# Order of VectorE's work in the seven-product up stage of a hybrid layer, with one operand kept in DRAM a second time

## The chip, the cores and the metric

The kernel runs on one core of a Trainium2 chip. The metric is the device time of one execution in microseconds (us), as the median of several runs; lower is better. TensorE (PE) multiplies matrices into PSUM; VectorE (DVE), ScalarE (ACT) and GpSimd (POOL) work element by element; SyncE (SP) issues most of the transfers between DRAM and on-chip memory (SBUF). Each engine works through its own list of instructions in a fixed order; where an instruction needs the result of another engine, it waits, and everything behind it on that engine waits too.

## What is computed

One decoder layer on 512 tokens of width 1024: two token mixers side by side (RWKV-7 time mixing and a sparse attention), gates, an output projection, and then a gated MLP. The change lies in the MLP, which is the last part:

```python
h = rms_norm(x, norm_ffn_pre[l])
u = causal_dwconv(h @ ffn_up[l], ffn_conv_w[l], ffn_conv_b[l])
u_gate, u_val = jnp.split(u, 2, axis=-1)
x = x + rms_norm((jax.nn.silu(u_gate) * u_val) @ ffn_down[l], norm_ffn_post[l])
```

`ffn_up` is 1024 x 5632, `ffn_down` 2816 x 1024; the convolution goes over three neighbouring tokens of each channel.

## The kernel before, in words

**Precision.** Each float32 operand of a product is split into a high part (rounded by a ScalarE copy to the matmul's format) and a low part (operand minus high part, one subtraction). A product is then three matmuls: high by high, low by high, high by low. So every weight tile costs a load (SP), a copy (ACT) and a subtraction (POOL or DVE: `split_to`, L166 to L172), and every activation tile a copy and a subtraction.

**The up stage** (L1593 to L1652) runs over 22 steps j, each of which makes 128 gate channels and 128 value channels of `u` for all 512 tokens, then the product y = silu(gate) * value, whose high part goes to `ah[:, j]` (L1638, ACT) and whose low part goes to `al[:, j]` (L1639, DVE). For j = 0 to 9 a step is two plain products. For j = 10 to 21 (`SEVEN`) the function `seven(j)` computes the 2 x 2 block product of a step with seven half-size products instead of eight. Each of the seven (`prod`, L1562) is 12 matmuls of 256 columns, and takes one weight tile from the list `ahead`. They go into the accumulators `sg` (gate), `sv` (value) and two temporary ones `st` (`t[0]`, `t[1]`), all in PSUM, and VectorE combines them between the products (`add`, L1571, whose line all the combining rows of the profile carry).

Two of the seven share `t[1][:, rgt]`: the fourth product is written there, VectorE reads it in `add(v[:, rgt], t[1][:, rgt], u4)` (L1584), and the seventh product, with `forms[3]` (L1587), is then accumulated on top of it. So TensorE may not start the seventh product of a step before that addition is done. The text calls this addition **the gate**; in the profile it is the first `sv<-st,su` of a step, and TensorE's row behind it is the first `st<-tf3h`.

**Weights of the seven products.** `form_w` (L1538) loads a tile, makes its high part and its low part. Of the seven tiles of a step five have their low part on POOL, and two on VectorE: the ones whose names end in 1 (`sw171`) and in 8 (`sw178`); the digits in front are the j. `coming` makes one more tile after each product, five tiles ahead of TensorE (L1615).

**What comes behind a step.** y's step runs on while the products of the next j are under way: convolution on ACT and DVE (L1619 to L1621), silu, y (L1635), `ah`, `al`. The down stage does the same trick with seven products over 2 x 2 blocks: its steps pair channel block j with block j + 11 (`KH` = 11). For j < 11 the right half of y is replaced by right minus left (L1637); the text calls that half T1 of block j. For j >= 11 VectorE also makes two token sums of 256 columns each and stores them in `t24d`: y's right half minus T1, and y's left half minus that. T1 is put together again from its two parts, so that the first sum takes two instructions: minus the high part (L1647), minus the low part (L1648); L1649 is the second sum.

**What sets the order.** The kernel's code gives the program order; a scheduling layer orders the instructions of each engine by it and by its own estimates, except where `keep` (keep in program order) pins an instruction. The buffers are rings: a load into a ring's slot waits until its last reader is done.

**The down stage** (L1655 on) works through 77 weight tiles `dw0` to `dw76`; the first ten are begun ahead of it. The raw tile of `dw8` and `dw9` lies in the pool `t2`, those from `dw10` on mostly in the pool `ep` in the tag `draw`.

Of the kernel before, what the change touches and what calls it, by code (L numbers as in the profile page):

```python
# [52 lines left out]
def hybrid_layer(ctx: ExitStack, tc: tile.TileContext, a, out, dbg=None, stop=None):  # L53
# [207 lines left out]

    t24d = dr.tile([KH, 128, S], F32, name="t24d", bufs=1)
# [1216 lines left out]
    with pool("ff") as ff:  # L1479
# [58 lines left out]
        def form_w(src, name, eng):  # L1538
            n = next(ring)
            p_, tags, b = (wp, ("raw", "whi", "wlo"), (RAWB, WB)) if n % 8 % 3 == 1 else (sw, ("sraw", "shi", "slo"), (4, 5))  # L1540
            hi = p_.tile([128, 512], F32R, tag=tags[1], name=name + "h", bufs=b[1])
            lo = p_.tile([128, 512], F32R, tag=tags[2], name=name + "l", bufs=b[1])
            split_to(src, hi, lo, name, 512, eng, p_, late=n < 5, tag=tags[0], bufs=b[0])
            return hi, lo

# [12 lines left out]
        def seven(j):  # L1558
# [3 lines left out]
            def prod(p, x, first=True, last=True):  # L1562
# [6 lines left out]
                next(coming, None)  # L1569

# [13 lines left out]
            add(v[:, rgt], t[1][:, rgt], u4)  # L1584
            prod(g[:, rgt], tok(1, 1))
            add(g[:, rgt], g[:, rgt], u4, OP.subtract)
            prod(t[1][:, rgt], forms[3], first=False)  # L1587
            add(v[:, lft], t[1][:, rgt], u2)
            return g, v

        side = token_forms()
        sctx2 = ExitStack()
        for j in range(22):  # L1593
# [45 lines left out]
            ve.tensor_tensor(al[:, j, :], y, ah[:, j, :].bitcast(F32), op=OP.subtract)  # L1639
            if j >= KH:  # L1640
                if j == KH:
                    t2ctx = ExitStack()
                    t2 = pool("t2", "left", t2ctx)
                else:
                    sy.dma_start(t24d[j - 1 - KH], t24)
                t24 = t2.tile([128, S], F32, tag="t24", name=f"t24{j}", bufs=2)
                ve.tensor_tensor(t24[:, lft], y[:, rgt], ah[:, j - KH, rgt].bitcast(F32), op=OP.subtract)  # L1647
                ve.tensor_tensor(t24[:, lft], t24[:, lft], al[:, j - KH, rgt].bitcast(F32), op=OP.subtract)  # L1648
                ve.tensor_tensor(t24[:, rgt], y[:, lft], t24[:, lft], op=OP.subtract)  # L1649
            if j == 1:  # L1650
                f4ctx.close()
        po.dma_start(t24d[21 - KH], t24)  # L1652
        ring = itertools.count()

        def down_w(f, k):  # L1655
# [8 lines left out]
            elif n < 10:  # L1664
                raw = t2.tile([128, 512], F32, tag="draw", name=f"dw{n}r", bufs=2)
            else:
                raw = ep.tile([128, 512], F32, tag="draw", name=f"dw{n}r", bufs=4)
# [12 lines left out]
        with pool("ep") as ep:  # L1680
# [3 lines left out]
            g3 = ep.tile([128, D], F32, name="gb4")  # L1684
            s2, x2 = {}, {}
# [233 lines left out]
```

## Time and profile before

| | |
|---|---|
| median of 3 runs | 1137.9 us (1136.57 to 1139.19) |
| the profiled execution: its time, and the span of its trace | 1133.54 us, 1131.5 us |
| granted TensorE clock, mean | 0.997 |
| busy share of the span: PE, DVE, ACT, POOL | 98%, 66%, 56%, 54% |
| DMA: moved, mean rate | 208.33 MB, 184 GB/s |

The page of the profile gives per engine the busy time; the groups of instructions by line, engine and tile (`sw171l<-sw171r,sw171h` is the low part of tile sw171, made from the raw tile and its high part); the waits (who waited, for whom); the chain of work that ended last; and, on request, the instructions in order of time and the busy times in any stretch. Times within the trace count from the start of the span. A row of the timeline has start, duration, engine, line, operation, tiles and shape, and in brackets the idle time ahead of it with what ended it. Rows of VectorE overlap by some 0.08 us, since the next instruction starts before the last one has drained; what an instruction costs its engine is the distance from its start to the next start.

### The profile page before, as it was taken

The numbers are of one execution on the slowest core, as the hardware profiler recorded it, in microseconds if no ns is written. First come the engines' busy times: TensorE is split into PE (matmuls) and PEld (weight loads), VectorE is DVE, ScalarE is ACT, GpSimd is POOL, SyncE is SP. The second block draws the span as 40 slices with busy tenths as digits, with TensorE's granted clock in tenths as the row PEclk, the third lists the DMA queues.
The fourth block names the chain that finished last, engine by engine and source line by source line (L and its number), as shares of the span: only waits on it lengthen the run. The fifth ranks groups of instructions, "written<-read, shape, count | busy, mean of one in ns | idle before, by whom it ended". The sixth has DMA issues, their size and how long they took to land.

```text
span 1131.5 us, 21237 instructions
## 1 busy us (share of the span) xinstructions
PE 1110.3 (98%) x7704; PEld 909.6 (80%) x7704; DVE 750.4 (66%) x1432; ACT 639.2 (56%) x1258; POOL 613.5 (54%) x615
## 2 busy tenths in 40 slices
PE   9999999999999999999999999999999999999997
PEld 7888888877888887766666777888888899998885
DVE  4236664735666552597787754755785699997986
ACT  6447763554666434386675654543554576665554
POOL 4346674535666453566545543540578777753431
PEclk9999999999999999999999999999999999999999
DMA  7524468632666896516576465777568678968783
GB/s 256 144 81 124 141 166 217 182 104 86 182 146 172 235 242 216 132 48 194 171 218 181 127 149 166 231 240 220 136 185 202 207 263 227 266 181 302 228 283 113
DMA packets 117002, 208.33 MB, mean 184 GB/s; under 512 B 37025, under 2 KB 39905, under 8 KB 110754
## 3 DMA queue, kind: packets, MB, share of 16 engines
q1 hardware_dynamic: 93538, 144.05, 40.6%
q0 software_dynamic: 7504, 48.50, 18.4%
q10 hardware_dynamic: 15856, 14.42, 4.0%
q8 instruction: 61, 1.00, 0.4%
q14 instruction: 43, 0.35, 0.1%
HBM read 179.60 MB, written 72.35 MB: 223 GB/s over the span
## 4 chain that ended last, share of the span: by engine, by line
PE 87%; DVE 5%; DMA 3%; POOL 2%; issue 1%; ACT 1%; SPq 0%; DVEq 0%; POOLq 0%; ACTq 0%
PE st L1567 4%; PE sg L1567 3%; PE dn L1745 3%; PE dn L1746 3%; PE dn L1747 3%; PE gt L348 3%; PE o L1218 3%; PE gt L349 3%; PE gt L350 3%; PE pt L150 3%; PE ub L1276 3%; PE pu L234 2%; PE ub L1278 2%; PE pu L232 2%; PE pu L233 2%; PE ub L1277 2%
## 5 line engine op out<-in xcount | busy, mean ns | idle before, releaser
L1166 ACT ACTIVATE p<-p,stt 128x384 f32<-128x384 f32 (+3 forms) x128 | 70.6, 554 | 33.4 <-DVE stt L1164 30.8
L1164 DVE CUSTOM_DVE_ANT_0 p<-s,rh 128x384 f32<-128x384 f32 (+3 forms) x128 | 59.2, 484 | 21.5 <-PE s L1150 17.9
L1138 POOL TENSOR_SCALAR p<-p,stt 128x512 f32<-128x512 f32 (+1 forms) x64 | 39.3, 622 | 38.7 <-DVE stt L1131 24.5
L1746 PE MATMUL dn<-hl,ah 128*128 128x512 f32 x148 | 57.6, 389 | 0.0
L1747 PE MATMUL dn<-hh,al 128*128 128x512 f32 x148 | 57.6, 389 | 0.0
L1745 PE MATMUL dn<-hh,ah 128*128 128x512 f32 x148 | 57.2, 389 | 0.0
L150 PE MATMUL pt<-ident,p 128*128 128x128 f32 x320 | 44.3, 273 | 1.2 <-DVE p L1140 1.2
L1157 PE MATMUL s<-kst,qs 128*128 128x512 f32 (+1 forms) x128 | 38.8, 394 | 5.8 <-DVE stt L1164 5.6
L150 PEld LDWEIGHTS pt<-ident,p 128*128 128x128 f32 x320 | 37.8, 141 | 6.9 <-DVE p L1140 1.6
L1218 PE MATMUL o<-PT,vt 128*64 128x384 f32 (+3 forms) x256 | 41.0, 443 | 0.0
L1209 ACT ACTIVATE PT<-pt 128x512 f32<-128x512 f32 x48 | 27.5, 587 | 10.4 <-PE pt L150 10.3
L1157 PEld LDWEIGHTS s<-kst,qs 128*128 128x128 f32 x128 | 21.2, 189 | 15.0 <-DVE stt L1164 11.8
L1140 DVE TENSOR_SCALAR p<-p,stt 128x512 f32<-128x512 f32 (+1 forms) x64 | 32.3, 532 | 0.7
L1747 PEld LDWEIGHTS dn<-hh,al 128*128 128x128 f32 x148 | 27.8, 188 | 5.8
L1745 PEld LDWEIGHTS dn<-hh,ah 128*128 128x128 f32 x148 | 27.8, 188 | 5.8
L1746 PEld LDWEIGHTS dn<-hl,ah 128*128 128x128 f32 x148 | 27.8, 188 | 5.7
L1218 PEld LDWEIGHTS o<-PT,vt 128*64 128x64 f32 x256 | 16.3, 136 | 18.3 <-issue 16.0
L272 POOL DMA_DIRECT2D ds<-in_down_dram x36 | 25.6, 710 | 7.3 <-DMA ds<-ds 7.3
L1620 DVE SCALAR_TENSOR_TENSOR u<-pu,cvec,u 128x511 f32<-128x511 f32 x20 | 15.0, 748 | 19.2 <-ACT u L1619 19.2
L1211 DVE COPY PT<-pt 128x512 f32<-128x512 f32 x32 | 21.8, 680 | 8.6 <-PE pt L150 8.5
L251 POOL DMA_DIRECT2D fs<-in_up_dram x36 | 26.0, 731 | 0.5 <-issue 0.4
L868 ACT ACTIVATE UV<-xs 64x256 f32<-64x256 f32 x16 | 6.0, 378 | 35.7 <-PE xs L861 35.3
(2206 smaller groups left out, 4242.4 us busy)
## 6 DMA issues: line engine op xcount, KB each, us to landing
fs<-in_up_dram POOLq DMA_DIRECT2D x36, 512.0 KB, 6.5
ds<-in_down_dram POOLq DMA_DIRECT2D x30, 512.0 KB, 6.1
fs<-fs POOLq DMA_DIRECT2D x12, 512.0 KB, 4.4
ds<-ds POOLq DMA_DIRECT2D x10, 512.0 KB, 5.7
gtd<-gt ACTq DMA_DIRECT2D x16, 256.0 KB, 4.8
qs<-qd SPq DMA_DIRECT2D x32, 128.0 KB, 3.6
g<-gtd SPq DMA_DIRECT2D x16, 256.0 KB, 3.6
t24d<-t SPq DMA_DIRECT2D x10, 256.0 KB, 5.4
```

Source lines behind the costliest of these rows:

```text
L150: return te.transpose(o, i, ident)
L348: te.matmul(p, wh(k), hh[:, k, :], start=k == 0, stop=False)
L349: te.matmul(p, wh(k), hl[:, k, :], start=False, stop=False)
L1138: po.tensor_scalar(o.pe[e, b, k], o.pe[e, b, k], w, 1.0, op0=OP.mult, op1=OP.mult)
L1157: m = te.matmul(s_[:, :n], qt, kt[:, x, b, :n], start=x == 0, stop=x == 1)
L1164: ve.tensor_tensor_reduce(sb, parts[b], rh[e][:, (3 - qb) * 128:], -1.0, BIG, OP.add, OP.min, st[e][:, 0, i:i + 1])
L1166: sc.activation(sb, sb, AF.Exp, scale=-1.0, bias=st[e][:, 0, i:i + 1], accum_out=st[e][:, 1, i:i + 1])
L1218: te.matmul(acc[e * 64:e * 64 + 64, j * 128:], vt[:, j, b * 256 + g * 64:b * 256 + g * 64 + 64], m[e][:, c:c + n], start=False, stop=k == ...
L1567: te.matmul(p, w[y][:, ks], x[z][:, k, :], start=first and k + n == 0, stop=last and k == hf - 1 and n == 2, skip_group_check=True)
L1745: te.matmul(p, xh, w[0], start=first, stop=False)
L1746: te.matmul(p, xh, w[1], start=False, stop=False)
L1747: te.matmul(p, xl, w[0], start=False, stop=last)
```

## The change

- `form_w`: where a low part is VectorE's, the load and the high part are issued as before, but the low part is put on a list `lows`; `flush()` issues what is on it. `flush` is called twice in a step: behind the gate and behind the last reader of `t[1]`.
- `al` and the token sums of a step are put on a list `deferred`. `settle()` issues them, in the next step behind the gate; where the step is not one of `SEVEN`, or is the last, at once.
- T1 of each block j < 11 is also stored in float32 in a DRAM buffer `t1d` (a store of 128 KB on ACT's queue), and loaded again by SP into a ring of two tiles `t1`, two blocks ahead of its use. The first token sum is then one instruction, y's right half minus this tile.
- `coming` makes one tile more per product in j = 10, until seven tiles are ahead.
- The raw tiles of `dw8` and `dw9` lie in the pool `sw` instead of `t2`; in `ep` the tile `p2jk` is laid out ahead of `draw`, so that the `draw` tiles lie elsewhere.

```diff
@@ form_w
-            split_to(src, hi, lo, name, 512, eng, p_, late=n < 5, tag=tags[0], bufs=b[0])
+            if n < 5 or eng is po:
+                split_to(src, hi, lo, name, 512, eng, p_, late=n < 5, tag=tags[0], bufs=b[0])
+            else:
+                raw = p_.tile([128, 512], F32, tag=tags[0], name=name + "r", bufs=b[0])
+                sy.dma_start(raw, src)
+                sc.activation(hi, raw, AF.Copy)
+                lows.append((lo, raw, hi))
             return hi, lo
+
+        lows = []
+
+        def flush():
+            while lows:
+                lo, raw, hi = lows.pop(0)
+                keep(ve.tensor_tensor(lo, raw, hi.bitcast(F32), op=OP.subtract))
@@ prod
                 next(coming, None)
+                if j == SEVEN[0] and len(ahead) < 7:
+                    next(coming, None)
@@ seven
             add(v[:, rgt], t[1][:, rgt], u4)
+            settle()
+            flush()
             prod(g[:, rgt], tok(1, 1))
             add(g[:, rgt], g[:, rgt], u4, OP.subtract)
             prod(t[1][:, rgt], forms[3], first=False)
             add(v[:, lft], t[1][:, rgt], u2)
+            flush()
             return g, v
+
+        hold, deferred = [], []
+
+        def t1_load(k):
+            t = hold[0].tile([128, 256], F32, tag="t1", name=f"t1{k}", bufs=2)
+            sy.dma_start(t, t1d[k])
+            return t
+
+        def settle():
+            while deferred:
+                j, y = deferred.pop(0)
+                ve.tensor_tensor(al[:, j, :], y, ah[:, j, :].bitcast(F32), op=OP.subtract)
+                if j >= KH:
...
+                    else:
+                        sy.dma_start(t24d[j - 1 - KH], hold[2])
+                    t24 = hold[2] = hold[0].tile([128, S], F32, tag="t24", name=f"t24{j}", bufs=2)
+                    ve.tensor_tensor(t24[:, lft], y[:, rgt], hold[3 + j - KH], op=OP.subtract)
+                    if j < 20:
+                        hold.append(t1_load(j - KH + 2))
+                    ve.tensor_tensor(t24[:, rgt], y[:, lft], t24[:, lft], op=OP.subtract)
@@ the loop over j
-            ve.tensor_tensor(al[:, j, :], y, ah[:, j, :].bitcast(F32), op=OP.subtract)
-            if j >= KH:
...
-                t24 = t2.tile([128, S], F32, tag="t24", name=f"t24{j}", bufs=2)
-                ve.tensor_tensor(t24[:, lft], y[:, rgt], ah[:, j - KH, rgt].bitcast(F32), op=OP.subtract)
-                ve.tensor_tensor(t24[:, lft], t24[:, lft], al[:, j - KH, rgt].bitcast(F32), op=OP.subtract)
-                ve.tensor_tensor(t24[:, rgt], y[:, lft], t24[:, lft], op=OP.subtract)
+            if j < KH:
+                tc.keep_in_program_order(sc.dma_start(t1d[j], y[:, rgt]))
+            deferred.append((j, y))
+            if sv_ is None or j == 21:
+                settle()
@@ down_w
-                raw = t2.tile([128, 512], F32, tag="draw", name=f"dw{n}r", bufs=2)
+                raw = sw.tile([128, 512], F32, tag="sraw", name=f"dw{n}r", bufs=4)
@@ the pool ep
+            ep.tile([128, 512], F32, tag="p2jk", name="p2jk", bufs=1)
```

TensorE's list is the same instruction for instruction. What moves stands here at two engines.

VectorE, before, while the products of j = 16 are under way and y of j = 15 is finished. `su` are the combining tiles u2 and u4 in SBUF, `t` is the token sum, the last two rows belong to the next turn:

```order
L1635 TENSOR_TENSOR sv_10748<-u_10890,sg_10747 128x512
L1572 TENSOR_TENSOR su_10908<-sv_10904,su_10907 128x256
L172 TENSOR_TENSOR sw171l<-sw171r,sw171h 128x512
L1639 TENSOR_TENSOR al<-sv_10748,ah 128x512
L1647 TENSOR_TENSOR t_10899<-sv_10748,ah 128x256
L1572 TENSOR_TENSOR sv_10904<-st_10906,su_10908 128x256
L1648 TENSOR_TENSOR t_10899<-t_10899,al 128x256
L1649 TENSOR_TENSOR t_10899<-sv_10748,t_10899 128x256
L1572 TENSOR_TENSOR sg_10903<-sg_10903,su_10908 128x256
L172 TENSOR_TENSOR sw178l<-sw178r,sw178h 128x512
L1620 SCALAR_TENSOR_TENSOR u_11041<-sg_10903,cvec,u_11041 128x511
```

VectorE, now, at the same place; L1588 is the line of `add`, L1620 that of `al`, L1630 and L1633 the token sums, L1558 the low parts:

```order
L1679 TENSOR_TENSOR sv_10773<-u_10922,sg_10772 128x512
L1588 TENSOR_TENSOR su_10934<-sv_10930,su_10933 128x256
L1620 TENSOR_TENSOR al<-sv_10773,ah 128x512
L1588 TENSOR_TENSOR sv_10930<-st_10932,su_10934 128x256
L1630 TENSOR_TENSOR t_11030<-sv_10773,t_10718 128x256
L1633 TENSOR_TENSOR t_11030<-sv_10773,t_11030 128x256
L1558 TENSOR_TENSOR sw171l<-sw171r,sw171h 128x512
L1588 TENSOR_TENSOR sg_10929<-sg_10929,su_10934 128x256
L1664 SCALAR_TENSOR_TENSOR u_11074<-sg_10929,cvec,u_11074 128x511
L1588 TENSOR_TENSOR sv_10930<-st_10932,su_10933 128x256
L1558 TENSOR_TENSOR sw178l<-sw178r,sw178h 128x512
```

Ahead of the gate (`sv<-st,su`) the low part of sw171 and the first token sum are gone, and `al` still stands there. One of the three token instructions is gone. The low part of sw178 has gone behind the second `sv<-st,su`, so that nothing stands any more between `sg<-sg,su` and the convolution's first instruction on `sg`.

SyncE, before, around the store of a token sum:

```order
L168 DMA sw164r<-fs_129 128x512
L168 DMA sw162r<-fs_127 128x512
L168 DMA sw163r<-fs_128 128x512
L168 DMA sw175r<-in_up_dram 128x512
L1645 DMA t24d<-t_10587 128x512
L168 DMA sw173r<-fs_128 128x512
L168 DMA sw166r<-in_up_dram 128x512
```

SyncE, now:

```order
L168 DMA sw164r<-fs_129 128x512
L168 DMA sw162r<-fs_127 128x512
L168 DMA sw175r<-in_up_dram 128x512
L1614 DMA t_10718<-t1d 128x256
L1628 DMA t24d<-t_10716 128x512
L168 DMA sw163r<-fs_128 128x512
L168 DMA sw166r<-in_up_dram 128x512
L168 DMA sw173r<-fs_128 128x512
```

The load of T1 stands directly ahead of the store; the load of sw163 has gone behind both.

More of the change, by code (lines that the diff above doesn't have):

```diff
@@ L260, in weight_sums @@
                     yield
+    t1d = dr.tile([KH, 128, 256], F32, name="t1d", bufs=1)
     t24d = dr.tile([KH, 128, S], F32, name="t24d", bufs=1)
@@ L1588, in seven @@
             add(v[:, lft], t[1][:, rgt], u2)
+            flush()
             return g, v
+        hold, deferred = [], []
[8 more added lines that the diff above has]
+                if j >= KH:
+                    if j == KH:
+                        t2ctx = ExitStack()
+                        hold[:] = [pool("t2", "left", t2ctx), t2ctx, None]
+                        t1s = hold + [t1_load(0), t1_load(1)]
+                        hold[:] = t1s
+                    else:
[5 more added lines that the diff above has]
+                    ve.tensor_tensor(t24[:, rgt], y[:, lft], t24[:, lft], op=OP.subtract)
         side = token_forms()
@@ L1638, in hybrid_layer @@
             sc.activation(ah[:, j, :], y, AF.Copy)
-            ve.tensor_tensor(al[:, j, :], y, ah[:, j, :].bitcast(F32), op=OP.subtract)
-            if j >= KH:
[L1641 to L1645, printed above, removed]
-                t24 = t2.tile([128, S], F32, tag="t24", name=f"t24{j}", bufs=2)
-                ve.tensor_tensor(t24[:, lft], y[:, rgt], ah[:, j - KH, rgt].bitcast(F32), op=OP.subtract)
-                ve.tensor_tensor(t24[:, lft], t24[:, lft], al[:, j - KH, rgt].bitcast(F32), op=OP.subtract)
-                ve.tensor_tensor(t24[:, rgt], y[:, lft], t24[:, lft], op=OP.subtract)
+            if j < KH:
[3 more added lines that the diff above has]
+                settle()
             if j == 1:
                 f4ctx.close()
+        t2, t2ctx, t24 = hold[:3]
         po.dma_start(t24d[21 - KH], t24)
```

## The prediction

> **What bounds the kernel now.** I read the page first: which engine is full.
>
> ```profile
> PE 1110.3 (98%) x7704; PEld 909.6 (80%) x7704; DVE 750.4 (66%) x1432; ACT 639.2 (56%) x1258; POOL 613.5 (54%) x615
> ```
>
> TensorE is the bound, and its work isn't changed. An edit on VectorE can only bring what TensorE loses by waiting in that stage. So next come the busy times in stretches: first the steps of the stage, each cut at TensorE's first matmul of a step (j = 10 starts at 898.91), then the whole stage and the down stage. Behind each stretch stand its length, the busy time of PE, its weight loads, DVE, ACT and POOL with the number of instructions, TensorE's clock, the DMA engines' share and GB/s.
>
> ```profile
> 898.91:908.63 9.72, 9.72 (x85) 9.71 (x84) 7.92 (x12) 6.31 (x11) 7.22 (x6) 1.00 0.78 244
> ...
> 928.15:937.84 9.69, 9.69 (x87) 9.69 (x85) 9.23 (x17) 6.94 (x13) 7.08 (x6) 1.00 0.80 256
> ...
> 968.19:978.82 10.63, 10.02 (x86) 9.82 (x85) 10.28 (x17) 7.30 (x14) 8.18 (x7) 1.00 0.93 262
> 978.82:988.50 9.68, 9.68 (x86) 9.68 (x85) 8.54 (x17) 6.55 (x13) 5.33 (x5) 1.00 0.93 266
> ...
> 898.91:1018.99 120.08, 118.40 (x1009) 117.51 (x1008) 111.97 (x185) 80.27 (x141) 84.04 (x68) 1.00 0.79 235
> 1018.99:1121.20 102.21, 102.21 (x453) 84.65 (x452) 85.12 (x100) 58.47 (x102) 37.99 (x25) 1.00 0.70 239
> ```
>
> The first four steps take (937.84 - 898.91) / 4 = 9.73 us, which is TensorE's own pace, 1.39 for each of the seven products. Twelve would take 116.8; the stage takes 120.08. So 3.3 us are lost, at a clock of 1.00, in the steps from j = 14 on; with the shortest step, 9.68, it would be 120.08 - 116.2 = 3.9. This is the most that the change can bring. The down stage loses nothing. VectorE is busy for 112 of the 120 us: a few tenths more per step and it is the bound. Who holds TensorE up stands in the waits and in TensorE's rows at j = 16:
>
> ```profile
> PE st L1567 <- DVE sv L1572: 1.6, 3, 0.7
> 964.73 0.28 PE L1567 MATMUL sg<-hh,sw164h 128*128 128x256 f32 x1
> 966.05 0.28 PE L1567 MATMUL sg<-hh,sw164l 128*128 128x256 f32 x1
> 966.68 0.39 PE L1567 MATMUL st<-tf3h,sw168h 128*128 128x256 f32 x1 [0.35 <-DVE sv L1572]
> ```
>
> The seventh product should follow at 966.17 and starts at 966.68, behind the gate. What VectorE did until then:
>
> ```profile
> 959.62 0.42 DVE L1572 TENSOR_TENSOR sv<-st,su 128x256 f32<-128x256 f32 x1
> 959.95 0.73 DVE L1621 SCALAR_TENSOR_TENSOR u<-sg,cvec,u 128x510 f32<-128x510 f32 x1
> 960.88 0.75 DVE L1620 SCALAR_TENSOR_TENSOR u<-sv,cvec,u 128x511 f32<-128x511 f32 x1 [0.20 <-ACT u L1619]
> ...
> 962.66 0.69 DVE L1635 TENSOR_TENSOR sv<-u,sg 128x512 f32<-128x512 f32 x1
> 963.26 0.42 DVE L1572 TENSOR_TENSOR su<-sv,su 128x256 f32<-128x256 f32 x1
> 963.59 1.76 DVE L172 TENSOR_TENSOR sw171l<-sw171r,sw171h 128x512 fp32r<-128x512 f32 x1
> 965.27 0.68 DVE L1639 TENSOR_TENSOR al<-sv,ah 128x512 fp32r<-128x512 f32 x1
> 965.88 0.41 DVE L1647 TENSOR_TENSOR t<-sv,ah 128x256 f32<-128x256 f32 x1
> 966.21 0.41 DVE L1572 TENSOR_TENSOR sv<-st,su 128x256 f32<-128x256 f32 x1
> 966.54 0.41 DVE L1648 TENSOR_TENSOR t<-t,al 128x256 f32<-128x256 f32 x1
> 966.98 0.42 DVE L1649 TENSOR_TENSOR t<-sv,t 128x256 f32<-128x256 f32 x1
> 967.32 0.42 DVE L1572 TENSOR_TENSOR sg<-sg,su 128x256 f32<-128x256 f32 x1
> 968.27 1.37 DVE L172 TENSOR_TENSOR sw178l<-sw178r,sw178h 128x512 fp32r<-128x512 f32 x1 [0.53 <-ACT sw178h L134]
> 969.57 0.73 DVE L1620 SCALAR_TENSOR_TENSOR u<-sg,cvec,u 128x511 f32<-128x511 f32 x1
> 970.23 0.41 DVE L1572 TENSOR_TENSOR sv<-st,su 128x256 f32<-128x256 f32 x1
> ```
>
> The gate (966.21) could have run at 963.6: the fourth product was done by 963.4, since the fifth and sixth, 1.39 each, come behind it. Ahead of it stand a low part of 1.68, `al` and a token sum. The whole turn, 959.62 to 970.23, is 10.61 us, longer than TensorE's 9.73. The gate ends at 966.62, when TensorE has been waiting since 966.17.
>
> **The change part by part.** The code puts `al`, the token sums and the low part behind the gate; in the list as it comes out the low part and the sums are behind it, and `al` is not. I lay out VectorE's new turn with the distances between these starts. Rows that stay: the second `sv<-st,su` .33; convolution and u2 from 959.95 to 962.66, 2.71 less the wait of .20 (the low part of sw178, now ahead of them, fills it) = 2.51; y .60; u4 .33; `al` .61; gate .33; two token sums .67; `sg` .33; convolution on `sg` .66. Sum 6.37.
>
> *Two waits come in*, both for ACT. One is at `al`, since sw171 no longer fills the time of `ah`; the other is at the convolution on `sg`, which now follows `sg<-sg,su` directly. The rows that show such times:
>
> ```profile
> 963.38 0.60 ACT L1638 ACTIVATE ah<-sv 128x512 fp32r<-128x512 f32 x1 [0.18 <-DVE sv L1635]
> 998.63 0.42 DVE L1572 TENSOR_TENSOR sg<-sg,su 128x256 f32<-128x256 f32 x1
> 999.91 0.75 DVE L1620 SCALAR_TENSOR_TENSOR u<-sg,cvec,u 128x511 f32<-128x511 f32 x1 [0.26 <-ACT u L1619]
> ```
>
> `ah` ends at 963.98; with .05 for the signal (.03 between y's end at 963.35 and `ah`) `al` starts at 964.03, and VectorE is free at 963.59: a wait of .44. From `sg` to its convolution ACT's copy takes 999.91 - 998.63 = 1.28, of which .33 is `sg` itself: a wait of .95. Behind both waiting instructions stands all of VectorE's list, the gate behind the first. With them the turn is 7.76 and the two low parts. The wait of .53 for sw178's high part goes: it ended at 968.25, before the new place of its low part.
>
> *The two low parts* decide, and this trace gives them two prices:
>
> ```profile
> 898.91:1018.99 120.08, 26.36 (x23) 76.33 (x56) 1.00 0.79 235
> L1647 DVE TENSOR_TENSOR t<-sv,ah x10: 406/408/416, 924.4 to 1017.9; 128x256 f32<-128x256 f32 x10
> L1648 DVE TENSOR_TENSOR t<-t,al x10: 407/426/1514, 925.1 to 1018.4; 128x256 f32<-128x256 f32 x10
> ```
>
> The first row is the low parts' line in the stage, VectorE's and POOL's: 26.36 / 23 = 1.15 us each on VectorE, 1.07 from start to start. Undisturbed one costs .60, like `al`; beside a running low part of POOL 1.68 or 1.30, as quoted. POOL is at them for 76 of 120 us, so that the new place won't be free of it. The token rows show the same thing: with one operand in PSUM (L1647) the time never moves, with both in SBUF (L1648) it goes to 1514 ns. The Trainium skill, page "SBUF — State Buffer", section "Who interferes with whom", speaks against this change: an instruction with two SBUF inputs contends with GpSimd's reads wherever it stands, and whoever starts first holds the shared port to the end. The 1514 agrees with that. By this rule, with POOL always first, each low part would take .60 + 1.30 and the turn 11.6, an estimate; the row's 1.15 tells that POOL is first less than half the time.
>
> The removed sum is L1648; the new first sum reads y from PSUM and the T1 tile, as L1647 read `ah`: .41, and at most the 1.51 of L1648. I take .41, the row of the same operands.
>
> So the new turn is 7.76 + 2 x 1.07 = 9.90; 8.96 with both undisturbed, 10.74 with 1.68 and 1.30. Against TensorE's 9.73 it grows late by .17 a step. The budget: a turn that follows TensorE starts its `sg` .05 behind the sixth product, that is 1.39 - .05 before the next step, and its second `sv` 1.28 + .66 later, .60 into the step. The gate comes .33 + 1.07 + 2.51 + .60 + .33 + .44 + .61 = 5.89 later and takes .41: it ends 6.90 into the step. TensorE needs it after six products, 6 x 1.39 = 8.34. That leaves 1.4 us of slack. Ten steps of .17 use 1.7, so that the last one or two wait, .3 in all; I add .2 for TensorE's late restarts behind a wait. Loss left: .5 instead of 3.3, a gain of 2.8.
>
> *The low parts come later* by about 2 us. What covers that is the lead of the weights. A narrow one of this trace is sw164, delayed by a late transfer:
>
> ```profile
> 958.99 1.52 POOL L172 TENSOR_TENSOR sw164l<-sw164r,sw164h 128x512 fp32r<-128x512 f32 x1
> SPq L1645 <- DVE sg L1572: 7.1, 6, 1.9
> L521 ACTq DMA_DIRECT2D gtd<-gt x16: 326/326/356, 164.6 to 384.4; - x16
> t24d<-t SPq DMA_DIRECT2D x10, 256.0 KB, 5.4
> ```
>
> It was ready at 960.51 and used at 964.73, 4.2 us ahead; sw171, done at 965.35, is used in the step that starts at 968.19. Cost 0; without cover it is us for us.
>
> *The traffic.* Each store of T1 costs ACT .33 to issue, like the stores in the third row, and ACT is free for 40 of 120 us: 0, at most .33 for j = 10. Each load costs SP about the same, and it waits for VectorE's token sum, with the weight loads queued behind it. The store of `t24d`, which stands at that place now, already waits so, 7.1 us in six times (second row), and the sums come no later. In the stage 11 x 128 KB are 1.4 MB more, 6 us at 235 GB/s spread over 120: .79 becomes .84 of the DMA engines. I take 0, because of the lead of 4 us; at worst 6.
>
> *Down stage.* `dw8` and `dw9` load later, once their slots' low parts are done, before 1018.99. `dw8` is due after eight tiles of six matmuls, 48 x 102.21 / 453 = 10.8 us later; a transfer of that size (5.4, last row), a high part (.6, as `ah`) and a low part on POOL (1.5, sw164) take 7.5. The new places in `ep` change whose end a load waits for, not the lead. Cost 0.
>
> **Sum.** In the profiled execution 1133.54 - 2.8 = 1130.7. The median of the runs, 1137.9, is 4.4 above that execution; what these lie apart in isn't in the trace, so I keep it and get 1135.1.
>
> **The rivals.** (1) *Half the gain*: one low part in two is held up, 1.68 + .60 = 2.28, the turn 10.04, late by .31 a step: 3.1 - 1.4 = 1.7 lost, gain 1.6, 1136.3. For it: the mean of 1.15 lies as near to the disturbed rows as to the undisturbed, and VectorE now often starts just behind ACT. Chance .20.
>
> (2) *Slower: POOL holds the port at both low parts.* Place: the new slots behind the gate and behind the second `sv`. Price as in the quoted turn, 1.68 + 1.30: turn 10.74, late by 1.01 a step, 10.1 - 1.4 = 8.7 lost instead of 3.3, 1143.3. It decides once the two cost more than 2.44 together (a turn of 10.20, where .47 x 10 - 1.4 = 3.3). Against it: that their start beside POOL's came from high parts that ACT finished just before, and the new places aren't tied to these. By the rule of the Trainium skill's page named above it happens whenever POOL starts first. Chance .10.
>
> (3) *No change*: the order on the chip moves, but the loads slip by what VectorE wins, since raw slots come free 2 us later and traffic is up by 5%; 1137.9. For it: the longest step quoted has a DMA share of .93. Against it: so has the shortest, and what TensorE waited for was `sv`, not a weight. Chance .10.
>
> **How the numbers follow.** The forecast has .60. A measurement here tells about 0.2%, 2.3 us, from no change. Of the forecast's .60 I put .52 beyond that bound, since 2.8 is just above it and runs spread by 1 us; with .02 of rival 1 faster is .54. Slower is rival 2 and .02 of rival 3, .12; the rest, .34, is within. The range: below, all 3.9 gone and .7 for the spread of runs, 1133.3; above, rival 3 and .8 of spread, 1138.7. Rival 2 is left out.
>
> **What would show it.** Right: the twelve steps take 116.8 to 117.5 us; no row of TensorE's seventh product waits for `sv`; the gate starts 1 us or more before the sixth product ends; VectorE waits .4 at `al` and .9 at the first convolution. Wrong: long steps remain, with low parts at 1.7 behind the gate (rivals 1, 2), or with ACT waiting for weight loads (rival 3), or a down stage above 102.2.

## The result, and the profile after

The change made the kernel slower: 1146.5 us (median of 6 runs, 1144.05 to 1149.69) against 1136.9 for the kernel before on the same chip (6 runs, 1131.92 to 1139.19), a ratio of 1.0087 with an interval of 1.0062 to 1.0113. That is 9.5 us more; 2.8 less were forecast. The profiled execution took 1146.39 us, its span 1144.4.

The engines' row on the page after:

```profile
PE 1117.9 (98%) x7704; PEld 914.4 (80%) x7704; DVE 742.7 (65%) x1421; ACT 640.2 (56%) x1258; POOL 615.5 (54%) x615
```

VectorE's work has become shorter by 7.7 us (750.4 before), and yet the kernel is slower. The stretches after, some steps first, then the whole stage and the down stage:

```profile
902.35:912.34 9.99, 9.99 (x85) 9.84 (x84) 8.20 (x10) 5.72 (x10) 7.44 (x7) 1.00 0.72 231
912.34:922.29 9.95, 9.95 (x86) 9.91 (x85) 8.64 (x15) 6.80 (x12) 7.88 (x7) 1.00 0.83 266
922.29:933.76 11.47, 10.05 (x86) 9.85 (x85) 10.14 (x17) 6.70 (x12) 7.33 (x7) 1.00 0.71 224
...
943.54:955.30 11.76, 10.18 (x87) 9.98 (x85) 8.65 (x16) 6.81 (x12) 7.34 (x7) 1.00 0.85 223
955.30:969.53 14.23, 11.25 (x87) 11.06 (x85) 9.24 (x18) 7.47 (x13) 8.83 (x8) 0.88 0.76 212
969.53:980.78 11.25, 11.25 (x85) 11.25 (x85) 9.05 (x15) 7.16 (x12) 7.77 (x7) 0.85 0.90 253
...
902.35:1031.82 129.47, 122.08 (x1010) 120.71 (x1008) 104.77 (x175) 80.36 (x141) 85.07 (x68) 0.97 0.79 233
1031.82:1134.03 102.21, 102.11 (x451) 84.22 (x450) 85.70 (x98) 58.45 (x101) 37.72 (x26) 1.00 0.70 241
```

The stage takes 129.47 instead of 120.08, 9.4 us more, which is what the medians differ by; the down stage takes 102.21 as before. (The two profiled executions lie 12.9 us apart, since the stage starts 3.4 us later in this one. That start moves from 898.0 to 905.3 among the runs below, with and without the change.) The loss comes in single long steps, the first at j = 12, and not as a small lag in each. TensorE itself is busy 3.7 us longer (122.08 against 118.40), at a mean clock of 0.88 and 0.85 in j = 15 and 16; the rest is waiting. Who waited, after, for whom (sum, times, longest), and then VectorE's largest such row before:

```profile
PE st L1581 <- DVE sv L1588: 7.4, 4, 3.0
DVE u L1664 <- ACT u L1663: 15.6, 12, 3.8
DVE al L1620 <- ACT ah L1682: 8.4, 11, 3.2
```
```profile
DVE u L1620 <- ACT u L1619: 3.0, 11, 0.8
```

TensorE waits for the gate 7.4 us instead of 1.6, and 5.8 + 3.7 are the 9.4 of the stage within the rounding. VectorE, with 7.2 us less work in the stage (104.77 against 111.97), now waits 15.6 + 8.4 = 24.0 us for ScalarE; its work and these waits are 128.8 of the 129.47. At the longest wait, in j = 15, the rows of SP, ACT, DVE and PE are:

```profile
956.23 1.36 SPq L168 DMA_DIRECT2D sw163r<-fs  x1
964.57 0.63 ACT L134 ACTIVATE sw163h<-sw163r 128x512 fp32r<-128x512 f32 x1 [3.53 <-DMA sw163r<-fs]
965.10 0.58 ACT L1682 ACTIVATE ah<-sv 128x512 fp32r<-128x512 f32 x1
965.72 0.69 DVE L1620 TENSOR_TENSOR al<-sv,ah 128x512 fp32r<-128x512 f32 x1 [3.16 <-ACT ah L1682]
966.32 0.42 DVE L1588 TENSOR_TENSOR sv<-st,su 128x256 f32<-128x256 f32 x1
966.80 0.58 PE L1581 MATMUL st<-tf3h,sw158h 128*128 128x256 f32 x1 [2.98 <-DVE sv L1588]
```

A weight load lands 8.3 us after its issue (the same tile before: 3.0); ScalarE waits for it and keeps `ah` behind it; `al`, the gate and TensorE follow. This chain gave the first theory.

### The profile page after: what moved, and what is told of

Its sections match the earlier page's. It is cut to its first block, busy times and chain, and to the rows that moved or that the text cites. A ratio compares the mean times of both kernels' runs of the same rounds, so it can differ in the third digit from the quotient of the medians.

```text
span 1144.4 us, 21284 instructions
## 1 busy us (share of the span) xinstructions
PE 1117.9 (98%) x7704; PEld 914.4 (80%) x7704; DVE 742.7 (65%) x1421; ACT 640.2 (56%) x1258; POOL 615.5 (54%) x615
## 4 chain that ended last, share of the span: by engine, by line
PE 76%; DVE 9%; DMA 7%; issue 3%; ACT 3%; POOL 2%; SPq 0%; DVEq 0%; ACTq 0%; POOLq 0%
PE o L1219 3%; PE pt L150 3%; PE gt L349 3%; PE ub L1277 3%; PE ub L1279 2%; PE gt L351 2%; PE gt L350 2%; PE ub L1278 2%; PE pu L234 2%; PE pu L232 2%; PE pu L233 2%; PE v L349 2%; PE v L350 2%; PE v L351 2%; PE dn L1786 2%
## 5 line engine op out<-in xcount | busy, mean ns | idle before, releaser
L1165 DVE CUSTOM_DVE_ANT_0 p<-s,rh 128x384 f32<-128x384 f32 (+3 forms) x128 | 59.2, 484 | 23.2 <-PE s L1151 19.5
L1219 PEld LDWEIGHTS o<-PT,vt 128*64 128x64 f32 x256 | 16.7, 139 | 19.0 <-issue 16.9
```

The lines of the kernel that those rows point to most:

```text
L1165: ve.tensor_tensor_reduce(sb, parts[b], rh[e][:, (3 - qb) * 128:], -1.0, BIG, OP.add, OP.min, st[e][:, 0, i:i + 1])
L1219: te.matmul(acc[e * 64:e * 64 + 64, j * 128:], vt[:, j, b * 256 + g * 64:b * 256 + g * 64 + 64], m[e][:, c:c + n], start=False, stop=k == ...
```

## The experiments

Each ratio is to runs of the kernel before on the same chip (medians of 1135.45 to 1136.65 us); the stage and the waits are those of the profiled execution.

### T1, its ring, and SyncE's order

Theory S: on SyncE the load of T1 and the store of the sums, which wait for VectorE's sums, now stand ahead of the load of tile 3 (sw163), and the loss feeds itself. Rival T: T1's loads or traffic; rival L: the new places of the low parts.

```diff
# e1_no_t1: the kernel after, T1 not kept in DRAM
-            t1s = hold + [t1_load(0), t1_load(1)]
-            ve.tensor_tensor(t24[:, lft], y[:, rgt], hold[3 + j - KH], ...)
+            ve.tensor_tensor(t24[:, lft], y[:, rgt], ah[:, j - KH, rgt], ...)
+            ve.tensor_tensor(t24[:, lft], t24[:, lft], al[:, j - KH, rgt], ...)
```

> The kernel after without T1 in DRAM: neither its stores nor its loads, and the first token sum in two instructions again. The low parts, al and the sums stay held back, with seven tiles ahead. On SyncE the store of the token sums still stands ahead of the load of the tile whose name ends in 3. Theory S (in SyncE's queue something that waits for VectorE's late sums stands ahead of a weight load, ScalarE then waits for that weight ahead of ah, and al, gate and sums come later still): the store alone is enough, since it waits for the same sums; the stage stays at 126 to 131 us, the time at 1143 to 1148, and ScalarE still waits for weight loads 153 or 163. Rival T (it is the T1 load and its traffic): the stage comes back to 117 to 120 us, 1134 to 1138. Rival L (the low parts' new places): as theory S in time, but VectorE is then late with no wait for ah.

Measured: 1153.25 us, 1.0160 (1.0129 to 1.0192), stage 135.29. Without T1 it is worse: T is out, and T1's shorter sum helps.

```diff
# e2_t1_only: the kernel before, with the buffers of the down stage as after
+            if j < KH:
+                tc.keep_in_program_order(sc.dma_start(t1d[j], y[:, rgt]))
-                ve.tensor_tensor(t24[:, lft], y[:, rgt], ah[:, j - KH, rgt].bitcast(F32), op=OP.subtract)
-                ve.tensor_tensor(t24[:, lft], t24[:, lft], al[:, j - KH, rgt].bitcast(F32), op=OP.subtract)
+                ve.tensor_tensor(t24[:, lft], y[:, rgt], t1s[j - KH], op=OP.subtract)
+                if j < 20:
+                    t1s.append(t1_load(j - KH + 2))
```

> The kernel before with T1 in DRAM alone: stores, loads into a ring of two, the first token sum in one instruction, the buffers of the down stage as after. Low parts, al and sums stay at their old places, five tiles ahead. Theory S: the sums are early, so a load or store that waits for them holds nothing up; the stage takes 119 to 121 us, the time 1136 to 1138. Rival T (T1's loads wait, or its traffic costs): the stage takes 126 us or more, 1143 to 1147. Rival L (low parts): as before, 1136 to 1138.

Measured: 1136.81 us, 1.0000 (0.9977 to 1.0022), stage 117.85. T1 costs nothing; in this execution the stage is 2.2 us shorter, but the medians show no gain.

```diff
# e4_ring4: the kernel after
-            t = hold[0].tile([128, 256], F32, tag="t1", name=f"t1{k}", bufs=2)
+            t = hold[0].tile([128, 256], F32, tag="t1", name=f"t1{k}", bufs=4)
# e8b_store_later: the kernel after; both transfers go on a list that is issued
# behind the second product of the next step
-            sy.dma_start(t24d[j - 1 - KH], hold[2])
+            later.append((t24d[j - 1 - KH], hold[2]))
```

> The kernel after with four T1 tiles instead of two, so that no load of T1 waits for VectorE; order as after on every engine. The store of the sums still waits for VectorE ahead of the weight load. Theory S with the store: nothing changes, stage 126 to 131 us, 1143 to 1148. If the T1 load's wait is what counts: 117 to 120 us, 1134 to 1138. Rival L: nothing changes.

Measured: 1150.70 us, 1.0133 (1.0107 to 1.0159), stage 130.60. No gain.

> The kernel after with the store of the token sums and T1's load issued later in the program, behind the second product of the next step; on SyncE the store then stands two to four weight loads later, behind the load of the tile that ends in 3, T1's load still ahead of it. Low parts as after. Theory S: the late weights are earlier, the stage 117 to 123 us, 1134 to 1140. Theory P or R: nothing changes, 126 to 131 us, 1143 to 1148.

Measured: 1143.91 us, 1.0084 (1.0060 to 1.0109), stage 126.78: the same as after. VectorE's wait at `al` falls from 8.4 to 3.8 us, so that the chain of theory S is gone, and the loss is not. SyncE's order is only half undone here: the store stands behind the load of sw153 but still ahead of that of sw163, and T1's load stays ahead of both. As the whole cause theory S fell with this.

### The low parts alone, and all but the low parts

```diff
# e3_lows_only: the kernel before, with form_w and flush of the kernel after
             add(v[:, rgt], t[1][:, rgt], u4)
+            flush()
...
             add(v[:, lft], t[1][:, rgt], u2)
+            flush()
```

> The kernel before with the low parts alone held back behind the gate and behind the second reader of the shared accumulator. al and the sums stay, no T1 in DRAM, five tiles ahead. SyncE's list has the load of tile 153 or 163 behind the store of the sums, as after. Theory S: the sums are as early as before, the store waits little; the stage takes 117 to 120 us, 1134 to 1138. Rival L (the new places of the low parts cost): 126 us or more, 1143 to 1147. Rival K (the mere order of the loads, the tile that ends in 3 behind the store): also 124 us or more, 1141 to 1147.

Measured: 1163.61 us, 1.0246 (1.0222 to 1.0271), stage 149.17. One part of the change alone costs 27 us, three times the whole change. In this kernel's timeline, VectorE's low part, POOL's beside it, and TensorE's row behind it:

```profile
956.62 3.56 DVE L1557 TENSOR_TENSOR sw148l<-sw148r,sw148h 128x512 fp32r<-128x512 f32 x1
```
```profile
956.92 1.49 POOL L172 TENSOR_TENSOR sw153l<-sw153r,sw153h 128x512 fp32r<-128x512 f32 x1
958.14 1.48 POOL L172 TENSOR_TENSOR sw154l<-sw154r,sw154h 128x512 fp32r<-128x512 f32 x1
```
```profile
960.24 0.39 PE L1580 MATMUL st<-tf3h,sw148l 128*128 128x256 f32 x1 [3.75 <-DVE sw148l L1557]
```

The 3.56 us (0.68 undisturbed) last until 0.56 behind the end of POOL's second low part. TensorE waits here for the held-back low part itself, which comes too late as a weight: some 18 of its 20 us of waiting in this stage are such waits, at the tile that ends in 8. The kernel after has none of them, all its 7.4 us are at the gate; so the 27 us are in the main another loss than the one to be explained.

The long row is theory P: POOL's low parts hold VectorE's up. Its rival R: a held-back low part frees its raw tile late, so that loads come late.

```diff
# e9_lows_back: the kernel after
-            if n < 5 or eng is po:
+            if True:
# e10_five_ahead: the kernel after
-                if j == SEVEN[0] and len(ahead) < 7:
-                    next(coming, None)
```

> The kernel after with the low parts at their old places; al and the token sums stay held back behind the gate, T1 stays in DRAM, seven tiles ahead, the buffers as after. On SyncE's list the load of the tile that ends in 3 is again ahead of T1's load and the store. Theory P or R (the held-back low parts are the cause, by POOL or by raw tiles that come free late): the stage comes to 117 to 121 us, 1133 to 1138. Theory S as first put (sums late, SyncE waits for them): 124 us or more, 1141 to 1147.

Measured: 1137.95 us, 1.0019 (1.0003 to 1.0035), stage 119.42. With the low parts at their old places most of the loss is gone (P or R).

> The kernel after with five tiles ahead as before instead of seven. On VectorE's list both low parts then stand next to each other behind the gate. Theory C and P: the weights' lead is shorter, loads that a late raw tile delays hit ScalarE and TensorE, as in the kernel with the low parts alone: slower than after, the stage 132 to 150 us, 1149 to 1165. If the lookahead is what costs: 118 to 124 us, 1135 to 1141.

Measured: 1163.35 us, 1.0240 (1.0216 to 1.0264), stage 148.17. The two further tiles are not the cost; they keep the change from costing 27 us. TensorE waits for the low part of the tile that ends in 8 here as in e3 (11.6 of 19.5 us). Since VectorE's list differs too, lead and place are not told apart here.

### POOL kept quiet

```diff
# q_before, q_after, q_lows_only: split_to in the kernels before, after and e3
-        (eng or po).tensor_tensor(lo, raw, hi.bitcast(F32), op=OP.subtract)
+        q = 16 if name.startswith("sw") and eng is po else n
+        (eng or po).tensor_tensor(lo[:, :q], raw[:, :q], hi[:, :q].bitcast(F32), op=OP.subtract)
+        if q < n:
+            po.memset(lo[:, q:].bitcast(F32), 0.0)
```

> The kernel before, in which POOL's low parts of the seven-product stage are left out but for 16 of 512 columns; the rest of each such tile is filled with zeros, which reads nothing from SBUF. So POOL still waits for each raw tile and its high part, but hardly reads beside VectorE. It is the control for the next kernel. Theory P (VectorE's low parts are slowed by POOL's): VectorE's low parts fall from 1.15 to 0.7 us each, its turn loses about 1 us a step, and the stage's loss of 3.3 us goes: 116 to 118 us, 1132 to 1135. Theory R (raw tiles come free too late) and S (SyncE's order): little changes, 118 to 121, 1135 to 1138.

Measured: 1132.94 us, 0.9976 (0.9960 to 0.9992), stage 118.45.

> The kernel after with the same left out: POOL's low parts of this stage but for 16 of 512 columns, zeros for the rest. Theory P: the low parts cost 0.7 us in their new places too, the turn is about 9.0, and the stage comes to 116 to 118 us, the time to 1132 to 1136. Theory R or S: ScalarE still waits for weight loads ahead of ah, VectorE for ah, and TensorE for the gate; the stage stays at 124 to 131 us, 1141 to 1147.

Measured: 1137.62 us, 1.0025 (1.0013 to 1.0038), stage 120.71. VectorE's low parts in the stage, the kernel after and then this one:

```profile
902.35:1031.82 129.47, 26.72 (x23) 0.97 0.79 233
```
```profile
902.17:1022.88 120.71, 15.60 (x23) 1.00 0.82 248
```

They fall from 1.16 to 0.68 us each. The change now costs 4.7 us (1137.62 - 1132.94) instead of 9.5: half of the loss needs POOL's reading.

> The kernel with the low parts alone held back (27 us slower than before), with POOL's low parts of the stage left out but for 16 of 512 columns and zeros for the rest, as in the two kernels with a quiet POOL. Theory P: most of the 27 us are POOL's, since a low part there takes up to 3.6 us: the stage falls from 149 to 119 to 126 us, the time to 1135 to 1141. Without P: the stage stays above 135 us, 1150 or more, by raw tiles that come free late and loads that ScalarE waits for.

Measured: 1145.97 us, 1.0083 (1.0059 to 1.0108), stage 128.36. Of 27 us 13 are left over the quiet kernel before (1145.97 - 1132.94). POOL is half here as well, short of the forecast of most of them (1135 to 1141). TensorE's waits for the low part itself are down to 1.9 us.

### One low part at a time

Theory C: the second half is lost cover. Where a low part stood between `sg<-sg,su` and the convolution on `sg`, or ahead of `al`, VectorE now waits for ScalarE, and each delay of ScalarE comes through.

```diff
# e11_hold1, e12_hold8: the kernel after
-            if n < 5 or eng is po:
+            if n < 5 or eng is po or name[-1] == "8":   # e11; e12 has "1"
```

> The kernel after in which only the low part of the tile that ends in 1 is held back behind the gate; that of the tile that ends in 8 stands where it stood before, between the subtraction on sg and the convolution on sg. Theory C (half of the loss is cover: with nothing between these two VectorE waits there 15.6 us in all for ScalarE; and the low part that ends in 8 costs 1.4 to 1.6 us in its new place): the wait falls below 8 us, the stage comes to 118 to 123 us, the time to 1135 to 1140. If the place behind the gate is what costs: 126 us or more, 1142 to 1147.

Measured: 1136.33 us, 1.0000 (0.9978 to 1.0022), stage 121.04.

> The kernel after in which only the low part of the tile that ends in 8 is held back, behind the second reader of the shared accumulator; that of the tile that ends in 1 stands ahead of the gate, and al and the sums now really stand behind the gate. Theory C: VectorE still waits 12 us or more for ScalarE at the convolution on sg; the stage takes 121 to 127 us, 1138 to 1144, worse than the kernel that holds the other one back. If the place behind the gate is what costs: 117 to 121 us, 1133 to 1138.

Measured: 1139.24 us, 1.0028 (1.0007 to 1.0049), stage 123.09. VectorE's waits at this convolution in e11 and in e12:

```profile
DVE u L1664 <- ACT u L1663: 2.8, 11, 0.8
```
```profile
DVE u L1664 <- ACT u L1663: 20.8, 13, 3.1
```

Over the kernel before, either low part alone costs 0 to 0.3% (with neither, e9, it is 0.2%), both together 0.9%: the two are not a sum.

```diff
# e13_gate_first: the kernel after, low parts at their old places, five tiles ahead
-            add(v[:, rgt], t[1][:, rgt], u4)
+            keep(ve.tensor_tensor(v[:, rgt], t[1][:, rgt], u4, op=OP.add))
             settle()
-                ve.tensor_tensor(al[:, j, :], y, ah[:, j, :].bitcast(F32), op=OP.subtract)
+                keep(ve.tensor_tensor(al[:, j, :], y, ah[:, j, :].bitcast(F32), op=OP.subtract))
```

> The kernel before with T1 in DRAM and its one-instruction sum, and with al and both sums behind the gate, in that order; both low parts at their old places, five tiles ahead, SyncE's and ScalarE's lists those of before but for T1. Theory C and P: the gate is 0.6 + 0.3 us earlier, one sum of 0.4 us is gone, and no cover is lost: the stage takes 117 to 119 us, 1133 to 1136. If al and the sums behind the gate are what costs: 122 us or more, 1139 or more.

Measured: 1136.81 us, 0.9993 (0.9970 to 1.0016), stage 122.44. The gate's earlier place brings nothing that can be measured.

### The open waits

```diff
# e14_ah_first (the kernel after), b14_ah_first (before), e16 (e11)
+        if name[:2] == "sw" and name[-1] == "3" and "ah" in last:
+            tc.add_manual_dep(i.ins, last["ah"].ins.name, ...)   # behind ah on ScalarE
# e18_sums_in_gap: the kernel after
             add(g[:, rgt], g[:, rgt], u4, OP.subtract)
+            sums()          # the two token sums, taken out of settle()
```

> The kernel after with one swap on ScalarE: ah stands ahead of the high part of the tile that ends in 3 instead of behind it; VectorE's list is the same, on SyncE a few loads change places. Theory C (ScalarE waits 3.5, 2.5 and 1 us for weight loads while ah is queued behind, and with the low parts gone VectorE has nothing else to do there): VectorE's wait at al falls from 8.4 us to 4 to 6, no gate is 2 us late, the stage takes 121 to 126 us, the time 1138 to 1143. If late loads don't matter and the low parts' collisions with POOL are all: 128 to 131 us, 1144 to 1148.

Measured: 1145.57 us, 1.0086 (1.0064 to 1.0108), stage 130.10. The wait at `al` (8.4 us, longest 3.2, in the kernel after) and two of VectorE's low parts:

```profile
DVE al L1624 <- ACT ah L1686: 3.8, 11, 0.4
L1562 DVE TENSOR_TENSOR sw188l<-sw188r,sw188h 128x512 fp32r<-128x512 f32 x1 | 3.8, 3765 | 0.0
L1562 DVE TENSOR_TENSOR sw148l<-sw148r,sw148h 128x512 fp32r<-128x512 f32 x1 | 3.7, 3656 | 0.0
```

The wait went as theory C said, and the time did not: two low parts now meet POOL for 3.7 us. The chain of j = 15 is thus real but not the cause by itself.

> The control: the same swap on ScalarE in the kernel before; VectorE's list is the same. Theory C: nothing to win, since before a low part of 1.7 us stands ahead of al and covers ah: stage 118 to 121 us, 1134.5 to 1138.

Measured: 1136.20 us, 1.0004 (0.9987 to 1.0022), stage 119.00, as expected of the control.

> The kernel after with the two token sums moved from behind the gate into the gap between the subtraction on sg and the convolution on sg; al stays behind u4, both low parts stay held back. If the open wait there costs time (theory C, what is left of it): the sums' 0.67 us a step run in time in which VectorE waits, its turn is 0.67 us shorter, the wait falls from 15.6 to 4 to 9 us, the stage takes 118 to 124 us, the time 1135 to 1141. If only the low parts' collisions with POOL count, since the gap is hidden elsewhere: 126 to 131 us, 1143 to 1148.

Measured: 1142.44 us, 1.0059 (1.0034 to 1.0084), stage 127.62. Some 3 us better than after (6 runs of 1139.13 to 1144.60 against 1144.05 to 1149.69; the intervals of the ratios overlap), less than forecast: the wait at the convolution fell from 15.6 to 13.6 us only, where 4 to 9 were forecast, and VectorE's low parts rose from 26.72 to 32.58 us.

`q_hold1` is e11 with the edit that keeps POOL quiet.

> The kernel that holds back only the low part of the tile that ends in 1, with POOL's low parts of the stage left out but for 16 of 512 columns and zeros for the rest. Theory C, what is left of it: without collisions the loss of the quiet kernel after (4.7 us over the quiet kernel before) is the open gap, so with the gap filled this kernel comes to the quiet kernel before: 1131 to 1135. If the rest of the change (sums, T1, seven tiles ahead, the place behind the gate) costs those 4.7 us: 1136 to 1139.

Measured: 1136.88 us, 1.0009 (0.9992 to 1.0025), stage 121.12. It does not come to the quiet kernel before; from the quiet kernel after (1.0025) it can't be told apart. So what the change costs without POOL's reading is not shown to be the gap, and stays open.

> The kernel that holds back only the low part of the tile that ends in 1 (1136.3, like before), with ah ahead of the high part of the tile that ends in 3. Theory C: its wait at al is already the round trip (3.8 us in all), so little is left to win: 117.5 to 120.5 us for the stage, 1133 to 1137. A gain beyond 0.2% would show at the gate: no wait of TensorE for it.

Measured: 1135.31 us, 0.9987 (0.9969 to 1.0004), stage 119.04. The best version, and not distinguishable from the kernel before.

## Why the prediction was wrong

**The bound** was read rightly: TensorE waited for the gate, and a few tenths more per step would make VectorE the bound. So was the removed work: VectorE's work in the stage fell to 104.77 us, where 12 turns of 9.90 less 1.39 of waiting, 102.1, were forecast, and the turn from 933.48 to 943.27, with no late weight in it, takes 7.84 without its low parts, against 7.76. T1's one-instruction sum, its traffic and the down stage cost nothing, as forecast.

Two terms of the turn's sum, "7.76 + 2 x 1.07 = 9.90", failed: both were taken as the same in every turn, and single turns decided.

**The first step that failed is the price of the two low parts, 2 x 1.07.** The mean held (1.15 forecast, 1.16 measured), but the price is not the same in each turn, and it is dearest in the first ones, which use up the slack of 1.4 us at once. VectorE's, POOL's and TensorE's rows after, in the first steps:

```profile
909.47 1.53 DVE L1558 TENSOR_TENSOR sw108l<-sw108r,sw108h 128x512 fp32r<-128x512 f32 x1
910.92 1.77 DVE L1558 TENSOR_TENSOR sw111l<-sw111r,sw111h 128x512 fp32r<-128x512 f32 x1
912.62 0.42 DVE L1588 TENSOR_TENSOR sg<-sg,su 128x256 f32<-128x256 f32 x1
913.89 0.75 DVE L1664 SCALAR_TENSOR_TENSOR u<-sg,cvec,u 128x511 f32<-128x511 f32 x1 [0.85 <-ACT u L1663]
...
914.88 1.41 DVE L1558 TENSOR_TENSOR sw118l<-sw118r,sw118h 128x512 fp32r<-128x512 f32 x1
916.22 0.73 DVE L1665 SCALAR_TENSOR_TENSOR u<-sg,cvec,u 128x510 f32<-128x510 f32 x1
...
921.07 1.01 DVE L1620 TENSOR_TENSOR al<-u,ah 128x512 fp32r<-128x512 f32 x1 [0.35 <-ACT ah L1682]
922.00 1.78 DVE L1558 TENSOR_TENSOR sw121l<-sw121r,sw121h 128x512 fp32r<-128x512 f32 x1
923.71 0.42 DVE L1588 TENSOR_TENSOR sg<-sg,su 128x256 f32<-128x256 f32 x1
...
931.76 0.42 DVE L1588 TENSOR_TENSOR sv<-st,su 128x256 f32<-128x256 f32 x1
...
932.88 0.68 DVE L1558 TENSOR_TENSOR sw131l<-sw131r,sw131h 128x512 fp32r<-128x512 f32 x1
```
```profile
914.45 1.30 POOL L172 TENSOR_TENSOR sw125l<-sw125r,sw125h 128x512 fp32r<-128x512 f32 x1
...
921.70 1.54 POOL L172 TENSOR_TENSOR sw124l<-sw124r,sw124h 128x512 fp32r<-128x512 f32 x1 [0.17 <-ACT sw124h L134]
```
```profile
932.24 0.39 PE L1581 MATMUL st<-tf3h,sw128h 128*128 128x256 f32 x1 [1.42 <-DVE sv L1588]
```

The same low parts before, with duration in ns behind the bar:

```profile
L172 DVE TENSOR_TENSOR sw118l<-sw118r,sw118h 128x512 fp32r<-128x512 f32 x1 | 1.3, 1285 | 0.2 <-ACT sw118h L134 0.2
L172 DVE TENSOR_TENSOR sw121l<-sw121r,sw121h 128x512 fp32r<-128x512 f32 x1 | 0.7, 678 | 0.0
```

Start to start the two cost 1.34 + 1.71 = 3.05 us in the turn from 912.62 to 923.71, which is 11.09 long; `al`, beside POOL too, takes 1.01 instead of 0.68. `sg` already comes late into this turn: it starts 0.28 behind the start of the step (912.34), where the forecast has it 1.34 ahead. That is 1.6 late, behind the two low parts of the turn before, which stand side by side and take from 909.47 to 912.62. 1.6 + (11.09 - 9.73) = 3.0; less the slack of 1.4 this makes 1.6, and TensorE waits 1.42 at 932.24. So the slack is gone after the first two turns, not after ten small lags. Once TensorE has waited, the engines stand differently to each other, and sw131 costs 0.68 again: a mean over the stage mixes turns that decide with turns that don't. Before, the first turns were the cheap ones. The first turn costs the same two prices, 1.33 to 1.37 and 1.70 to 1.73 start to start, in e1, e4, e8b, e11, e14 and e18. But this accounts for one of TensorE's four waits at the gate, 1.42 of 7.4 us.

POOL's 921.70 starts when ScalarE has just made the high part, and VectorE's new place behind the gate lies 0.30 later. The prediction argued that the new places "aren't tied to these" starts; at sw121 the two starts fell together all the same.

**Rival 2** (POOL at both low parts, decides beyond 2.44, 1143.3 us) was thus right in mechanism for the first turns, and near in time by luck. Only the pairs of the first two turns cost more than 2.44 (3.15 and 3.05; the others 1.3 to 2.4), and TensorE's three other waits came by another way. In e1 it went as rival 2 has it: nine of ten pairs cost 2.56 to 3.04, and TensorE waited 13.6 us at nine gates. The Trainium skill, page "SBUF — State Buffer", section "Who interferes with whom", says that an instruction with two SBUF inputs contends with GpSimd's reads, and not with its mere writes. The runs agree: 1.16 us beside POOL's subtractions, 0.68 beside its zero fills. That the first to start keeps the port is not what the rows of e3 show: there VectorE starts at 956.62, POOL's at 956.92 and 958.14, and VectorE ends last. (A row may begin before its instruction reads.)

**The two waits** were right in size where ScalarE was free (0.85 and 0.35 against 0.95 and 0.44), but taking them as constants, 16.7 us in twelve steps, is the second step that failed, and by the trace the larger one. 24.0 were measured; 3.1 of them lie at the convolution of j = 9, ahead of the first turn. In the turns all were 0.34 to 0.37 and 0.85 to 1.03 but three, of 2.12, 3.16 and 3.80, which are 7.3 us above the forecast. Three of TensorE's four waits at the gate follow just these, 1.58, 2.98 and 1.41, together 6.0 of 7.4 us. The first and the third, with ScalarE's row ahead of each (the second is j = 15, shown above):

```profile
951.54 0.63 ACT L134 ACTIVATE sw153h<-sw153r 128x512 fp32r<-128x512 f32 x1 [2.49 <-DMA sw153r<-fs]
952.69 0.69 DVE L1620 TENSOR_TENSOR al<-sv,ah 128x512 fp32r<-128x512 f32 x1 [2.12 <-ACT ah L1682]
953.78 0.39 PE L1581 MATMUL st<-tf3h,sw148h 128*128 128x256 f32 x1 [1.58 <-DVE sv L1588]
...
1011.20 0.63 ACT L134 ACTIVATE sw204h<-sw204r 128x512 fp32r<-128x512 f32 x1 [4.34 <-DMA sw204r<-fs]
1013.05 0.75 DVE L1664 SCALAR_TENSOR_TENSOR u<-sg,cvec,u 128x511 f32<-128x511 f32 x1 [3.80 <-ACT u L1663]
1020.31 0.38 PE L1581 MATMUL st<-tf3h,sw208h 128*128 128x256 f32 x1 [1.41 <-DVE sv L1588]
```

Each time ScalarE stands at a weight load. Why these loads land late stays open. The longest wait cost 3.4 us more through the clock, which was 0.50 for 6.8 us behind it (last section); no term of the sum stood for that.

**Together.** With the low part that ends in 8 at its old place (e11) two low parts still cost 1.4 and 1.8 in the first turns, but the wait of 0.85 is covered, and no loss can be measured. With the other one back (e12), 0.3%. Without POOL's reading, half. A collision or the open wait of 0.85 alone fits the slack of 1.4 us; both don't. A wait of 2 to 4 us doesn't fit it even alone, and costs more where low parts collide as well: 0.69 and 1.10 at the gate in the quiet kernel after, 1.41 to 2.98 in the kernel after. VectorE's own sum agrees: its work and its waits for ScalarE come to the length of the stage within 0.2 us in e1, e4, e8b, e12 and e18 (e12: 101.99 + 21.1 of 123.09), so that it waits for hardly anything else there; in e11 they come to 109.9 of 121.04, in e9 to 105.7 of 119.42, in the quiet kernel after to 118.3 of 120.71. This says that VectorE's turn is full, not why the long waits come.

The remaining 4.7 us of the quiet pair have no shown cause. In their profiled executions the stage makes 2.3 of the difference. There, and in q_hold1, each of TensorE's waits at the gate above 0.3 us (0.92; 0.69 and 1.10; 1.04, 0.87 and 1.63) follows a wait of VectorE for ScalarE of 2.4 to 3.8 us. That points to the late weights, and so to rival R among others, but no run with POOL quiet takes them away.

**"The traffic ... at worst 6" and rival 3** named weights that come late; the sum took them at 0, "because of the lead of 4 us". That lead is TensorE's. ScalarE comes to a tile earlier, waits for it in its own order, and holds `ah` or the convolution's copy back behind it. Changing SyncE's order in part (e8b) or ScalarE's (e14) shortened the wait at `al` in both to 3.8 us and brought nothing: long waits at the convolution (e8b: 3.7) or low parts of 3.7 us (e14) took their place.

**What the change could have won** is less than it seemed: e2, with a stage of 117.85 in its profiled execution, and e13 have the medians of the kernel before.

## What to carry to other kernels

Price an instruction that collides with another engine in the turn where it will stand, beside that engine's rows there, and not by its mean over a stage: the turns in which the bounding engine is still on time decide. Before moving work away from the front of a wait, count it as that wait's cover: two moves that each fit the slack can together exceed it. When a composite change loses, run each part alone early, and see which wait it makes: here one part alone lost three times as much as the whole, in the main by a wait that the whole doesn't have.

## What the runs showed of the hardware

A 128x512 float32 subtraction on VectorE with both operands in SBUF took 0.68 us alone, up to 2.4 beside one such instruction of POOL, and 3.3 to 3.8 beside two in a row. In the kernels before, after, e3, e10 and e14, each one that was held up ended 0.54 to 0.57 us behind the end of POOL's.

TensorE's mean clocks of 0.88 and 0.85 in the two steps around its wait of 2.98 us are a clock of 0.50 from 966.0 to 972.8 and of 1.00 elsewhere. Behind 3.17 us in e1, 2.18 in e4, 2.47 and 1.83 in e14 and 1.75 in e8b the clock was 0.50 for 3.4 us, which costs 1.7. In these kernels and the one after it stayed at 1.00 behind every wait of up to 1.68 us, and in e18 behind 1.78 and 1.91. So the length of a wait alone doesn't settle it.
